# Turning the attention's probabilities on VectorE, in blocks of 32 by 32, in a two-layer decoder trunk

## The chip, the core and the metric

The kernel runs on one core of a Trainium2 chip. The metric is the device time of one execution in microseconds (us), inputs and outputs in the chip's main memory. The kernel before takes 889.86 us, the median of three runs (889.71 to 890.35).

## The reference

One sequence of 512 tokens, width 1024, goes through two layers. The first mixes tokens by causal pooling over windows of 2, 4, 8 and 16 and has a gate. The second is attention with 16 heads of width 64 in three dilation branches (1, 4, 16) that share keys and values projected once; each branch gives an output and a log-denominator, and a softmax over those weighs the three. Each layer ends in a layer norm of `alpha * h + y`.

```python
scores = einsum('bnqrhd,bnkrhd->bnrhqk', qb, kk) * (HEAD_DIM ** -0.5)
scores = where(valid, scores - slope * dilation * rel, NEG_INF)
lse = logsumexp(scores, axis=-1)
p = exp(scores - lse[..., None])
out = einsum('bnrhqk,bnkrhd->bnqrhd', p, vv)          # per branch
...
wts = softmax(stack(lses), axis=0)
merged = sum(wts[..., None] * stack(outs), axis=0)
y = (merged * silu(gate)) @ w_out
```

Scores come out with queries on partitions and keys along the free dimension. The product with the values sums over keys, so the probabilities have to be turned, keys onto partitions, before it. That turning is what the change touches.

## The kernel before

Large products are done in three passes of a rounded type: each operand is split into `hi` and `lo`, and TensorE computes hi x hi, hi x lo and lo x hi (`project`, L526, matmuls at L534). For each weight tile of 128x1024, SyncE loads `raw`, ScalarE casts `hi` (L114) and VectorE subtracts `lo` (L115), with three buffers for each. One such projection of 128 output rows is 24 matmuls of 128x512. This text calls it a **fill**, because in the attention stage fills stand between the pieces of attention.

The attention stage works on 8 pairs of heads (`Attention`, two heads i = 0, 1). Each pair has two **kinds**: kind 0 is the branch of dilation 1, where a block of 128 queries meets the block of keys before it and its own, and kind 1 is the two dilated branches, where tokens are ordered by residue, so that each block of 128 queries meets 128 keys of its own block twice, once for each branch. In the branch of dilation 16 only the four blocks of 32 by 32 on the diagonal are not masked.

- `scores(kind)` (L601 on TensorE): 4 PSUM tiles `sc` of tag "sc" (4 buffers). VectorE's custom operation (L609) adds the mask to `sc`, writes `e` and its row minimum, 8 times; ScalarE takes the exponential in place and the sum (L613), 8 times. In kind 0 two of the eight cover 128 keys, the others 256.
- `transposed(kind, bb)`: turns `e`. In kind 0 TensorE transposes 6 (bb = 0) or 8 (bb = 1) squares of 128x128 into `tp` (L639) and ScalarE copies them to `eT` (L642). In kind 1 TensorE transposes the 4 squares of the branch of dilation 4 (L625), ScalarE copies them into `diag` (L626), and VectorE **turns** the diagonal blocks of the branch of dilation 16 with `transpose`, which turns each block of 32 by 32 (L630, four blocks in one operation).
- `values(kind)` (L655): the products with the values, into the PSUM tile `o`, copied by ScalarE to `o_sb`.
- `weigh` (VectorE; matmul `pm`), `turn` (transpose `ft`, `rows`, `rows_r`) and `spread` (two matmuls `fp`, L707, two multiplications of `o_sb` by `fp`, L709, and their sum `num`): the weights of the branches.

The PSUM tag "tp" has two buffers, and `tp`, `o` and `fp` take turns in them; an allocation waits until the tile two places earlier has been read. The orders of TensorE and SyncE are written out by hand; those of VectorE, ScalarE and GpSimd come from a scheduler that places each instruction by its own estimate of when it can run. Each engine runs its own queue in order. Step n of the loop below does: values of step n-2, scores of step n, then three fills, with the transposes of step n-1 between them and the pair's weights spread in the odd steps. A pair is two steps. The first 48 fills make keys and queries of all pairs and branches (`key_query`, L543; a `k` is copied from PSUM by ScalarE, L549, a `q` by VectorE with its scale, L552); the last 7 are gates, whose PSUM tile three VectorE passes read or follow (L565, L567, L570).

```python
for n in range(2 * NPAIR + 1):
    if n >= 2: heads[n // 2 - 1].values(n % 2)
    if n < 2 * NPAIR: heads[n // 2].scores(n % 2)
    next(fill)(done.turn if done else nothing)
    heads[(n - 1) // 2].transposed((n - 1) % 2, 0)
    next(fill)(nothing)
    heads[(n - 1) // 2].transposed((n - 1) % 2, 1)    # after kind 1: weigh()
    next(fill)(done.spread if done else nothing)
```

Of the kernel before, what the change touches and what calls it, by code (L numbers as in the profile page):

```python
# [8 lines left out]
F32 = mybir.dt.float32  # L9
F32R = mybir.dt.float32r  # L10
BF16 = mybir.dt.bfloat16
AF = mybir.ActivationFunctionType
# [3 lines left out]
P = 128  # L16
S = 512
# [3 lines left out]
NT = S // P  # L21
# [6 lines left out]
HD = 64  # L28
# [41 lines left out]
def trunk(ctx, tc, x, w_in_a, w_grp_a, scale_a, w_out_a, w_kv, w_in_b, w_out_b, ln_g, ln_b, tab, out):  # L70
    nc = tc.nc
    x = x[0]
# [11 lines left out]
    ps = ps_ab.enter_context(tc.tile_pool(name="ps_m", bufs=1, space=PSUM))  # L84
# [8 lines left out]
    ident = const.tile([P, P], F32, name="ident")  # L93
# [76 lines left out]
    with ExitStack() as pa:  # L170
# [135 lines left out]
        for half in range(2):  # L306
            acc = out_proj(ps_y, "y", 4, lambda k, tok: (a_hi[:, k, tok], a_lo[:, k, tok]), w_out_a, half)
            for t in acc:
                tok = slice(t * P, (t + 1) * P)
                h = layer_norm_rows(ap_, acc[t], xr[t], gb[:, 0], gb[:, 1])  # L310
                for kq in range(2):
                    tp = (ps, ps_y)[half].tile([P, 4, P], F32, name="tp", tag=("mm", "y")[half], bufs=4)
# [15 lines left out]
    with ExitStack() as pb:  # L328
# [4 lines left out]
        t_q, to_token, block, residue, qsc, row_block, spread_to = (tabs[:, e - n:e] for e, n in zip(ends, sizes))  # L333
# [4 lines left out]
        v_sb = [(v0s[p], v12s[p][:, 0], v12s[p][:, 1]) for p in range(NPAIR)]  # L338
# [176 lines left out]

        spread_r = qk.tile([P, 2, P], F32R, name="spread_r")
        nc.scalar.copy(spread_r, spread_to.rearrange("p (k m) -> p k m", k=2))
        diag = [qk.tile([P, 2, 2, 256], F32, name="diag", tag="diag", bufs=2) for _ in range(2)]
        for t in diag:
            nc.gpsimd.memset(t, 0.0)  # L520
        wide = []
        for _ in range(2):
# [20 lines left out]
        def key_query(pair, g, j):  # L543
            def emit(mid):
                pt = project((w_kv_v, w_in_v)[j][:, :, g * D + pair * P:g * D + (pair + 1) * P], mid)
                t = qk.tile([P, S], F32, name="kq"[j], tag="kq"[j], bufs=6)
                dst, src = shaped(g, t, pt)
                if j == 0:
                    nc.scalar.copy(dst, src)  # L549
                else:  # L550
                    c = 2 * pair + min(g, 1)
                    nc.vector.tensor_scalar_mul(dst, src, qsc[:, c:c + 1])  # L552
                kq[pair, g, j] = t
            return emit

# [18 lines left out]
        class Attention:  # L574
# [5 lines left out]
            def __init__(self, pair):  # L580
                self.pair = pair

                self.st = sm.tile([P, 2, NT, 4], F32, name="st", tag="st", bufs=2)
                self.own = sm.tile([P, NT, 4], F32, name="own", tag="own", bufs=2)
                self.e, self.eT, self.o = {}, {}, {}

            def scores(self, kind):
                pair = self.pair
                for bb in range(2):
                    sc = [ps_s.tile([P, 2, 256], F32, name="sc", tag="sc", bufs=4) for _ in range(2)]  # L590
                    first = [P * (kind == 0 and bb == 0 and j == 0) for j in range(2)]
                    for j in range(2):
                        b = 2 * bb + j
                        blk = slice(b * P, (b + 1) * P)
                        for g in ((0,), (1, 2))[kind]:
                            for i in range(2):
                                rows = slice(i * HD, (i + 1) * HD)
                                f = first[j]
                                dst, keys = ((sc[i][:, j, f:], slice((b - 1) * P + f, (b + 1) * P)) if g == 0 else
                                             (sc[i][:, j, (g - 1) * P:g * P], blk))  # L600
                                nc.tensor.matmul(dst, kq[pair, g, 1][rows, blk], kq[pair, g, 0][rows, keys],  # L601
                                                 start=True, stop=True)
                    stats = (self.st[:, 0], self.own)[kind]
                    self.e[kind, bb] = es = qk.tile([P, 2, 2, 256], F32, name="e", tag="e", bufs=4)
                    for i in range(2):
                        e = es[:, i]
                        for j in range(2):
                            b, f = 2 * bb + j, first[j]
                            nc.vector.tensor_tensor_reduce(  # L609
                                e[:, j, f:], sc[i][:, j, f:], t_q[:, kind * 256 + f:(kind + 1) * 256],  # L610
                                -SLOPES[2 * kind][2 * pair + i], 3e38, op0=ALU.add, op1=ALU.min,
                                accum_out=stats[:, b, i:i + 1])
                            nc.scalar.activation(e[:, j, f:], e[:, j, f:], AF.Exp, bias=stats[:, b, i:i + 1],  # L613
                                                 scale=-1.0, accum_out=stats[:, b, 2 + i:3 + i])

            def transposed(self, kind, bb):
                es = self.e.pop((kind, bb))
                if kind == 1:

                    t = diag[bb]  # L620
                    tp = ps.tile([P, 2, 2, P], F32, name="tp", tag="tp", bufs=2)
                    for i in range(2):
                        self.eT[kind, bb, i] = t[:, i].rearrange("p j c -> p (j c)")
                        for j in range(2):
                            nc.tensor.transpose(tp[:, i, j], es[:, i, j, 0:P], ident)  # L625
                    nc.scalar.copy(t.rearrange("p i j c -> p (i j) c")[:, :, 0:P], tp.rearrange("p i j c -> p (i j) c"))  # L626
                    for s in range(4):
                        q = slice(32 * s, 32 * (s + 1))
                        cols = slice(P + 32 * s, P + 32 * (s + 1))
                        nc.vector.transpose(t[q].rearrange("p i j c -> p (i j) c")[:, :, cols],  # L630
                                            es[q].rearrange("p i j c -> p (i j) c")[:, :, cols])
                    return
                for i in range(2):
                    e = es[:, i]
                    tp = ps.tile([P, S], F32, name="tp", tag="tp", bufs=2)

                    parts = [e[:, 0, P:], e[:, 1, 0:P], e[:, 1, P:]] + [e[:, 0, 0:P]] * bb
                    for c, part in enumerate(parts):
                        nc.tensor.transpose(tp[:, c * P:(c + 1) * P], part, ident)  # L639
                    n = len(parts) * P  # L640
                    self.eT[kind, bb, i] = t = qk.tile([P, S], F32, name="eT", tag="eT", bufs=4)
                    nc.scalar.copy(t[:, 0:n], tp[:, 0:n])  # L642

            def values(self, kind):
                o = ps.tile([P, S], F32, name=f"o{kind}", tag="tp", bufs=2)
                for bb in range(2):
                    b = 2 * bb

                    if kind == 0:
                        parts = [(0, b, 0, b, 2), (0, b + 1, 2, b + 1, 1)] + [(0, b - 1, 3, b, 1)] * bb  # L650
                    else:
                        parts = [(1 + g, b + j, 2 * j + g, b + j, 1) for j in range(2) for g in range(2)]
                    for n, (g, kb, c, qb, w) in enumerate(parts):
                        for i in range(2):
                            nc.tensor.matmul(o[i * HD:(i + 1) * HD, qb * P:(qb + w) * P], v_sb[self.pair][g][:, kb, i],  # L655
                                             self.eT[kind, bb, i][:, c * P:(c + w) * P],
                                             start=(bb == 0 and n == 0), stop=(bb == 1 and n == len(parts) - 1))
                self.o[kind] = o_sb = qk.tile([P, S], F32, name="o_sb", tag=f"o{kind}", bufs=1)
                if kind == 0:
                    nc.scalar.copy(o_sb, o)  # L660
                else:
                    nc.scalar.copy(o_sb.rearrange("p (a s r) -> p a s r", s=4, r=4),
                                   o.rearrange("p (r s a) -> p a s r", r=4, s=4))
# [27 lines left out]
            def turn(self):  # L691

                ft = ps_s.tile([P, S], F32, name="ft", tag="sc", bufs=4)
                nc.tensor.transpose(ft[:, 0:P], wide[self.pair % 2], ident)
                rows = qk.tile([P, NT, P], F32, name="rows", tag="rows", bufs=1)
                nc.vector.tensor_mul(rows, ft[:, 0:P].unsqueeze(1).broadcast_to([P, NT, P]),
                                     row_block.unsqueeze(2).broadcast_to([P, NT, P]))
                self.rows = qk.tile([P, NT, P], F32R, name="rows_r", tag="rows_r", bufs=1)
                nc.scalar.copy(self.rows, rows)
                nc.vector.tensor_sub(self.rows[32:48], rows[32:48], self.rows[32:48])  # L700
# [129 lines left out]
```

## Time and profile before

| | |
|---|---|
| median of the runs shown | 889.86 us |
| the profiled execution | 889.12 us, of which the trace's span is 887.3 |
| TensorE matmul busy | 876.3 us (99%), granted clock 0.999 |
| VectorE busy | 527.8 us (59%) |
| ScalarE busy | 369.4 us (42%) |
| GpSimd busy | 13.1 us (1%) |
| attention stage | from 441.7 us, one pair of heads every 43.80 us |

The rows further down come from six views. The page gives shares over the whole span; the windows give the busy time of each engine in one stretch; the chain in order of time says what the end waited for, piece by piece; the groups by form give the mean duration of one kind of instruction on one shape; and the timelines show instructions of one engine with their starts. TensorE's matmuls overlap, so the time that one costs is read from starts or from the chain's pieces, not from its duration. In the chain a piece counts records, and a product of two plain 32-bit operands leaves two records per instruction where `o` and `sc` are concerned.

### The profile page before, as it was taken

The page shows a single profiled execution, that of the slowest core. Times are in us where ns is not written, and L with a number is a line of the kernel's source. Part 1 is how long each engine was busy: PE and PEld are TensorE (multiplying, and loading weights), DVE is VectorE, ACT ScalarE, POOL GpSimd, SP SyncE. Part 2 cuts the span into 40 slices and gives each one's busy share as a digit, 9 for nine tenths or more (in the row PEclk, how much of TensorE's full clock was granted, in tenths as well). Part 3 has the DMA queues.
Part 4 walks back from the last instruction along what each step waited for, and adds up shares of the span by engine and source line. Part 5 has one row for each costly group of instructions (what it writes and reads, how often), then busy time and mean ns, then how long its engine had stood idle before and what let it go on. Part 6 is the DMA issues. An engine that isn't in the chain of part 4 may idle for free.

```text
span 887.3 us, 11570 instructions
## 1 busy us (share of the span) xinstructions
PE 876.3 (99%) x4499; PEld 717.2 (81%) x4499; DVE 527.8 (59%) x968; ACT 369.4 (42%) x699; POOL 13.1 (1%) x65
## 2 busy tenths in 40 slices
PE   9999999999999999999999999999999999999996
PEld 6888888888887877788888888888888888888885
DVE  3756466584549489879534454545454545465665
ACT  3633333333433425554543444444444444454410
POOL 0000000000000000000000000000000000000000
PEclk9999999999999999999999999999999999999999
DMA  7533434333455644352233222222222222223261
GB/s 226 177 96 96 144 94 148 103 104 98 142 193 188 217 164 138 119 168 66 64 107 95 72 72 72 72 72 72 72 73 72 72 72 72 72 72 95 72 214 71
DMA packets 112855, 97.70 MB, mean 110 GB/s; under 512 B 5152, under 2 KB 97312, under 8 KB 112800
## 3 DMA queue, kind: packets, MB, share of 16 engines
q1 hardware_dynamic: 112080, 94.39, 34.3%
q10 hardware_dynamic: 720, 2.57, 0.8%
q8 instruction: 35, 0.57, 0.3%
q14 instruction: 20, 0.16, 0.1%
HBM read 92.76 MB, written 4.19 MB: 109 GB/s over the span
## 4 chain that ended last, share of the span: by engine, by line
PE 94%; DVE 3%; issue 1%; ACT 0%; DMA 0%; DVEq 0%
PE mm L534 35%; PE y L145 9%; PE mm L127 6%; PE mm L126 6%; PE mm L128 6%; PE yb L729 5%; PE vy L468 4%; PE sc L601 3%; PE v L390 3%; PE o L655 3%; PE mm L224 3%; PE vz L468 2%; PE mx L126 2%; PE mx L127 2%; PE mx L128 2%; PE tp L639 1%
## 5 line engine op out<-in xcount | busy, mean ns | idle before, releaser
L115 DVE TENSOR_TENSOR lo<-raw,hi 128x1024 fp32r<-128x1024 f32 (+1 forms) x148 | 176.2, 1194 | 210.2 <-ACT hi L114 203.7
L114 ACT CAST hi<-raw 128x1024 fp32r<-128x1024 f32 (+1 forms) x148 | 151.7, 1029 | 307.8 <-issue 140.0
L534 PE MATMUL mm<-hi_T,hi 128*128 128x512 f32 x448 | 180.6, 403 | 0.0
L534 PE MATMUL mm<-hi_T,lo 128*128 128x512 f32 x448 | 175.3, 391 | 0.0
L534 PE MATMUL mm<-lo_T,hi 128*128 128x512 f32 x448 | 174.6, 390 | 0.0
L534 PEld LDWEIGHTS mm<-hi_T,hi 128*128 128x128 f32 x448 | 84.2, 188 | 20.3 <-issue 3.0
L534 PEld LDWEIGHTS mm<-hi_T,lo 128*128 128x128 f32 x448 | 84.1, 188 | 18.5
L534 PEld LDWEIGHTS mm<-lo_T,hi 128*128 128x128 f32 x448 | 84.4, 188 | 16.0
L127 PE MATMUL mm<-lo_T,hi 128*128 128x512 f32 x224 | 87.2, 389 | 0.0
L128 PE MATMUL mm<-hi_T,lo 128*128 128x512 f32 x224 | 87.2, 389 | 0.0
L126 PE MATMUL mm<-hi_T,hi 128*128 128x512 f32 x224 | 87.2, 389 | 0.0
L128 PEld LDWEIGHTS mm<-hi_T,lo 128*128 128x128 f32 x224 | 42.0, 188 | 8.8
L126 PEld LDWEIGHTS mm<-hi_T,hi 128*128 128x128 f32 x224 | 42.0, 188 | 8.8
L127 PEld LDWEIGHTS mm<-lo_T,hi 128*128 128x128 f32 x224 | 42.0, 188 | 8.6
L609 DVE CUSTOM_DVE_ANT_0 e<-sc,tabs 128x256 f32<-128x256 f32 (+1 forms) x128 | 43.3, 403 | 7.9 <-PE sc L601 7.9
L552 DVE TENSOR_SCALAR q<-mm,tabs 128x512 f32<-128x512 f32 x24 | 18.0, 751 | 46.2 <-PE mm L534 46.0
L145 PE MATMUL y<-lo,a_hi 128*128 128x512 f32 x128 | 39.9, 390 | 0.5 <-DVE lo L115 0.5
L145 PE MATMUL y<-hi,a_hi 128*128 128x512 f32 x128 | 39.9, 392 | 0.4 <-DVE x_tok L154 0.4
L145 PE MATMUL y<-hi,a_lo 128*128 128x512 f32 x128 | 39.7, 389 | 0.0
L729 PE MATMUL yb<-hi,a_b 128*128 128x512 f32 x128 | 39.7, 389 | 0.0
L359 DVE TENSOR_TENSOR lo<-b,hi 128x1024 fp32r<-128x1024 f32 x24 | 29.4, 1223 | 13.6 <-ACT hi L358 13.4
L358 ACT CAST hi<-b 128x1024 fp32r<-128x1024 f32 x24 | 25.3, 1055 | 26.1 <-PE vy L468 15.6
(175 smaller groups left out, 1329.1 us busy)
## 6 DMA issues: line engine op xcount, KB each, us to landing
raw<-in_w_out_a_dram SPq DMA_DIRECT2D x32, 512.0 KB, 3.3
raw<-in_w_kv_dram SPq DMA_DIRECT2D x32, 512.0 KB, 3.8
raw<-in_w_in_b_dram SPq DMA_DIRECT2D x32, 512.0 KB, 3.8
raw<-in_w_in_a_dram SPq DMA_DIRECT2D x28, 512.0 KB, 3.9
b<-in_w_kv_dram SPq DMA_DIRECT2D x16, 512.0 KB, 4.6
raw<-in_w_grp_a_dram SPq DMA_DIRECT2D x8, 512.0 KB, 3.6
raw<-in_w_out_b_dram SPq DMA_DIRECT2D x8, 512.0 KB, 3.3
x_col<-in_x_dram SPq DMA_DIRECT2D x4, 512.0 KB, 7.2
```

Of the source, the lines that this page charges most:

```text
L114: nc.scalar.copy(hi[:, parts[i]], raw[:, parts[i]])
L115: nc.vector.tensor_sub(lo[:, parts[i]], raw[:, parts[i]], hi[:, parts[i]])
L126: nc.tensor.matmul(ps, lh, rh, start=(i == 0), stop=False)
L127: nc.tensor.matmul(ps, lh, rl, start=False, stop=False)
L128: nc.tensor.matmul(ps, ll, rh, start=False, stop=(i == n - 1))
L145: nc.tensor.matmul(acc[t][c], l, r[:, 0, c * 512:(c + 1) * 512], start=(k == 0 and s == 0), stop=(k == nk - 1 and s == 2))
L224: nc.tensor.matmul(pts[i], l[:, kk, f], xT[r][:, k], start=(k == 0 and n == 0), stop=(k == NK - 1 and n == 2))
L359: nc.vector.tensor_sub(dst[1], src, dst[0])
L468: nc.tensor.matmul(acc[:, i], lhs[l][:, 2 * (n % 2) + kk, i], w[r][:, kk], start=(begins and kk == 0 and s == 0), stop=(n % 2 == 1 and kk ...
L534: nc.tensor.matmul(pt, l[:, k], hT[r][:, k], start=(k == 0 and n == 0), stop=(k == NK - 1 and n == 2))
L609: nc.vector.tensor_tensor_reduce(e[:, j, f:], sc[i][:, j, f:], t_q[:, kind * 256 + f:(kind + 1) * 256], -SLOPES[2 * kind][2 * pair + i], 3 ...
L729: nc.tensor.matmul(acc[t, c], a_b[k][:, l, tok], ws[k][r][:, 0, cs], start=(k == 0 and n == 0), stop=(k == NK - 1 and n == 2))
```

## The change

`e` and `eT` become four tiles that live through the whole stage, one of each per kind, with both heads and all four query blocks in them (128x2048). All squares are now turned by VectorE's `transpose` and written straight to `eT`. A helper `turn(q, k, ...)` takes the 32 partitions of block row q and the 32 columns of block column k, for all squares at once, turns each block and writes it to the 32 partitions k at the columns q. In kind 0 the first half turns the own-block squares with k <= q (10 operations over 8 squares), the second half the squares of the block before with k >= q (10 over 7). Blocks that the mask leaves empty are not turned; `eT` is cleared once by GpSimd. In kind 1 the 12 operations off the diagonal cover 8 squares of the branch of dilation 4, and the 4 on the diagonal cover both branches, 16. The tiles `tp` and `diag` go, with their transposes on TensorE and copies on ScalarE. The copy of a `q` from PSUM goes to ScalarE as an activation with a scale.

```diff
         spread_r = qk.tile([P, 2, P], F32R, name="spread_r")
         nc.scalar.copy(spread_r, spread_to.rearrange("p (k m) -> p k m", k=2))
-        diag = [qk.tile([P, 2, 2, 256], F32, name="diag", tag="diag", bufs=2) for _ in range(2)]
-        for t in diag:
+        e_t = [qk.tile([P, 2, NT, 256], F32, name="e", tag="e", bufs=2) for _ in range(2)]
+        eT_t = [qk.tile([P, 2, NT, 256], F32, name="eT", tag="eT", bufs=2) for _ in range(2)]
+        nc.gpsimd.memset(e_t[0][:, :, 0, 0:P], 0.0)
+        for t in eT_t:
...
                     nc.scalar.copy(dst, src)
                 else:
                     c = 2 * pair + min(g, 1)
-                    nc.vector.tensor_scalar_mul(dst, src, qsc[:, c:c + 1])
+                    nc.scalar.activation(dst, src, AF.Copy, scale=qsc[:, c:c + 1])
                 kq[pair, g, j] = t
...
                 self.own = sm.tile([P, NT, 4], F32, name="own", tag="own", bufs=2)
-                self.e, self.eT, self.o = {}, {}, {}
+                self.o = {}
             def scores(self, kind):
...
                     for i in range(2):
-                        e = es[:, i]
                         for j in range(2):
                             b, f = 2 * bb + j, first[j]
+                            e = e_t[kind][:, i, b, f:]
                             nc.vector.tensor_tensor_reduce(
-                                e[:, j, f:], sc[i][:, j, f:], t_q[:, kind * 256 + f:(kind + 1) * 256],
+                                e, sc[i][:, j, f:], t_q[:, kind * 256 + f:(kind + 1) * 256],
                                 -SLOPES[2 * kind][2 * pair + i], 3e38, op0=ALU.add, op1=ALU.min,
                                 accum_out=stats[:, b, i:i + 1])
-                            nc.scalar.activation(e[:, j, f:], e[:, j, f:], AF.Exp, bias=stats[:, b, i:i + 1],
+                            nc.scalar.activation(e, e, AF.Exp, bias=stats[:, b, i:i + 1],
                                                  scale=-1.0, accum_out=stats[:, b, 2 + i:3 + i])
-            def transposed(self, kind, bb):
-                es = self.e.pop((kind, bb))
+            def transposed(self, kind, half):
+                e, t = (x[kind].rearrange("p i b c -> p (i b) c") for x in (e_t, eT_t))
+                def turn(q, k, cols, rows, src, dst):
+                    q, k = (slice(32 * x, 32 * (x + 1)) for x in (q, k))
+                    nc.vector.transpose(dst[k][:, :, rows + q.start:rows + q.stop],
+                                        src[q][:, :, cols + k.start:cols + k.stop])
                 if kind == 1:
-                    t = diag[bb]
-                    tp = ps.tile([P, 2, 2, P], F32, name="tp", tag="tp", bufs=2)
-                    for i in range(2):
-                        self.eT[kind, bb, i] = t[:, i].rearrange("p j c -> p (j c)")
-                        for j in range(2):
-                            nc.tensor.transpose(tp[:, i, j], es[:, i, j, 0:P], ident)
-                    nc.scalar.copy(t.rearrange("p i j c -> p (i j) c")[:, :, 0:P], tp.rearrange("p i j c -> p (i j) c"))
-                    for s in range(4):
-                        q = slice(32 * s, 32 * (s + 1))
-                        cols = slice(P + 32 * s, P + 32 * (s + 1))
-                        nc.vector.transpose(t[q].rearrange("p i j c -> p (i j) c")[:, :, cols],
-                                            es[q].rearrange("p i j c -> p (i j) c")[:, :, cols])
+                    both = [x[1].rearrange("p i b (g c) -> p (i b g) c", g=2) for x in (e_t, eT_t)]
+                    for q in (2 * half, 2 * half + 1):
+                        for k in range(4):
+                            turn(q, k, 0, 0, *(both if q == k else (e, t)))
                     return
-                for i in range(2):
-                    e = es[:, i]
-                    tp = ps.tile([P, S], F32, name="tp", tag="tp", bufs=2)
-                    parts = [e[:, 0, P:], e[:, 1, 0:P], e[:, 1, P:]] + [e[:, 0, 0:P]] * bb
-                    for c, part in enumerate(parts):
-                        nc.tensor.transpose(tp[:, c * P:(c + 1) * P], part, ident)
-                    n = len(parts) * P
-                    self.eT[kind, bb, i] = t = qk.tile([P, S], F32, name="eT", tag="eT", bufs=4)
-                    nc.scalar.copy(t[:, 0:n], tp[:, 0:n])
+                for q in range(4):
+                    for k in range(4):
+                        if half == 0 and k <= q:
+                            turn(q, k, P, 0, e, t)
+                        elif half == 1 and k >= q:
+                            turn(q, k, 0, P, e[:, 1:], t[:, 0:-1])
             def values(self, kind):
                 o = ps.tile([P, S], F32, name=f"o{kind}", tag="tp", bufs=2)
-                for bb in range(2):
-                    b = 2 * bb
-                    if kind == 0:
-                        parts = [(0, b, 0, b, 2), (0, b + 1, 2, b + 1, 1)] + [(0, b - 1, 3, b, 1)] * bb
-                    else:
-                        parts = [(1 + g, b + j, 2 * j + g, b + j, 1) for j in range(2) for g in range(2)]
-                    for n, (g, kb, c, qb, w) in enumerate(parts):
-                        for i in range(2):
-                            nc.tensor.matmul(o[i * HD:(i + 1) * HD, qb * P:(qb + w) * P], v_sb[self.pair][g][:, kb, i],
-                                             self.eT[kind, bb, i][:, c * P:(c + w) * P],
-                                             start=(bb == 0 and n == 0), stop=(bb == 1 and n == len(parts) - 1))
+                if kind == 0:
+                    parts = [(0, 0, 0, 0, 2), (0, 1, 0, 1, 1), (0, 2, 0, 2, 2), (0, 3, 0, 3, 1), (0, 1, P, 2, 1)]
+                else:
+                    parts = [(1 + g, b, g * P, b, 1) for b in range(NT) for g in range(2)]
+                for n, (g, b, c, qb, w) in enumerate(parts):
+                    for i in range(2):
+                        nc.tensor.matmul(o[i * HD:(i + 1) * HD, qb * P:(qb + w) * P], v_sb[self.pair][g][:, b, i],
+                                         eT_t[kind][:, i, b, c:c + w * P],
+                                         start=(n == 0), stop=(n == len(parts) - 1))
                 self.o[kind] = o_sb = qk.tile([P, S], F32, name="o_sb", tag=f"o{kind}", bufs=1)
                 if kind == 0:
```

VectorE, a middle pair, from the last score operation of kind 1 to the multiplication by `fp` (rows of 128x1 are its sums). Before:

```order
453 L630 STREAM_TRANSPOSE diag<-e 32x4x32 x6
454 L696 TENSOR_TENSOR rows<-ft,tabs 128x512
455 L630 STREAM_TRANSPOSE diag<-e 32x4x32 x2
456 L669 TENSOR_TENSOR x<-own,tabs 128x64
457 L700 TENSOR_TENSOR rows_r<-rows,rows_r 16x512
458 L552 TENSOR_SCALAR q<-mm,tabs 128x512
459 L115 TENSOR_TENSOR lo<-raw,hi 128x1024 x2
460 L709 TENSOR_TENSOR o_sb<-o_sb,fp 128x512 x2
461 L711 TENSOR_TENSOR num<-o_sb 128x512
462 L552 TENSOR_SCALAR q<-mm,tabs 128x512
463 L115 TENSOR_TENSOR lo<-raw,hi 128x1024
```

VectorE, the same place in the new order, from `rows_r` on (ahead of these rows, behind the last score operation, stand one turn of 32x16x32, `rows` and three turns of 32x8x32):

```order
470 L696 TENSOR_TENSOR rows_r<-rows,rows_r 16x512
471 L625 STREAM_TRANSPOSE eT<-e 32x8x32
472 L625 STREAM_TRANSPOSE eT<-e 32x16x32
473 L625 STREAM_TRANSPOSE eT<-e 32x8x32
474 L115 TENSOR_TENSOR lo<-raw,hi 128x1024
475 L625 STREAM_TRANSPOSE eT<-e 32x8x32 x3
476 L625 STREAM_TRANSPOSE eT<-e 32x16x32
477 L625 STREAM_TRANSPOSE eT<-e 32x8x32 x4
478 L625 STREAM_TRANSPOSE eT<-e 32x16x32
479 L665 TENSOR_TENSOR x<-own,tabs 128x64
480 L115 TENSOR_TENSOR lo<-raw,hi 128x1024
481 L705 TENSOR_TENSOR o_sb<-o_sb,fp 128x512 x2
```

Eight turns of 32x4x32 stood ahead of `x`; now sixteen larger ones stand ahead of it, with one `lo` among them, and the copy of `q` that stood ahead of `lo` is gone. Both orders come to the multiplication of `o_sb` by `fp` after them.

TensorE, a middle pair, between the second and the third fill behind kind 1's scores, with tile numbers (`mm_4590` and `mm_4637` are the two fills). Before:

```order
L534 MATMUL mm_4590<-hi_T_1833,hi_4585 128x512
L534 MATMUL mm_4590<-lo_T_1834,hi_4585 128x512
L534 MATMUL mm_4590<-hi_T_1833,lo_4586 128x512
L639 MATMUL tp_4617<-ident_83,e_4329 128x128 x4
L639 MATMUL tp_4624<-ident_83,e_4329 128x128 x4
L534 MATMUL mm_4637<-hi_T_1833,hi_4632 128x512
L534 MATMUL mm_4637<-lo_T_1834,hi_4632 128x512
```

TensorE, the same place in the new order (fills `mm_4559` and `mm_4602`):

```order
L538 MATMUL mm_4559<-hi_T_1833,hi_4554 128x512
L538 MATMUL mm_4559<-lo_T_1834,hi_4554 128x512
L538 MATMUL mm_4559<-hi_T_1833,lo_4555 128x512
L538 MATMUL mm_4602<-hi_T_1833,hi_4597 128x512
L538 MATMUL mm_4602<-lo_T_1834,hi_4597 128x512
```

The transposes into `tp` that stood between the fills are gone, and nothing stands in their place.

VectorE, the last pair, where fills are gates (`sgb` and `a_b` are their tiles), up to the multiplication by `fp`. Before:

```order
733 L630 STREAM_TRANSPOSE diag<-e 32x4x32 x4
734 L700 TENSOR_TENSOR rows_r<-rows,rows_r 16x512
735 L669 TENSOR_TENSOR x<-own,tabs 128x64
736 L115 TENSOR_TENSOR lo<-raw,hi 128x1024
737 L565 SCALAR_TENSOR_TENSOR sgb<-sgb,mm 128x512
738 L567 SCALAR_TENSOR_TENSOR sgb<-num,sgb 128x512
739 L570 TENSOR_TENSOR a_b<-sgb,a_b 128x512
740 L115 TENSOR_TENSOR lo<-raw,hi 128x1024
741 L565 SCALAR_TENSOR_TENSOR sgb<-sgb,mm 128x512
742 L567 SCALAR_TENSOR_TENSOR sgb<-num,sgb 128x512
743 L709 TENSOR_TENSOR o_sb<-o_sb,fp 128x512
```

VectorE, the same place in the new order (ahead of it stand `rows`, two turns, `rows_r`, four turns and a `lo`):

```order
792 L569 SCALAR_TENSOR_TENSOR sgb<-sgb,mm 128x512
793 L625 STREAM_TRANSPOSE eT<-e 32x8x32
794 L571 SCALAR_TENSOR_TENSOR sgb<-num,sgb 128x512
795 L625 STREAM_TRANSPOSE eT<-e 32x8x32 x3
796 L574 TENSOR_TENSOR a_b<-sgb,a_b 128x512
797 L625 STREAM_TRANSPOSE eT<-e 32x16x32
798 L625 STREAM_TRANSPOSE eT<-e 32x8x32
799 L115 TENSOR_TENSOR lo<-raw,hi 128x1024
800 L569 SCALAR_TENSOR_TENSOR sgb<-sgb,mm 128x512
801 L625 STREAM_TRANSPOSE eT<-e 32x8x32
802 L571 SCALAR_TENSOR_TENSOR sgb<-num,sgb 128x512
803 L705 TENSOR_TENSOR o_sb<-o_sb,fp 128x512 x2
```

The passes of two gates stood ahead of the multiplication; now turns stand between them, and three more come after it.

## Rows read from the trace of the kernel before

**Rows 1.** The page: parts 1, 2 (clock by slice), 4 (chain).

```profile
PE 876.3 (99%) x4499; PEld 717.2 (81%) x4499; DVE 527.8 (59%) x968; ACT 369.4 (42%) x699; POOL 13.1 (1%) x65
...
PEclk9999999999999999999999999999999999999999
...
PE 94%; DVE 3%; issue 1%; ACT 0%; DMA 0%; DVEq 0%
```

**Rows 2.** Windows, two pairs of heads: us, then busy time by engine, clock.

```profile
678.80:722.60 43.80, 43.80 (x273) 35.86 (x274) 22.26 (x65) 20.34 (x51) 0.00 (x0) 1.00 0.25 73
...
766.40:810.20 43.80, 43.80 (x272) 35.86 (x273) 26.47 (x72) 23.21 (x56) 0.00 (x0) 1.00 0.25 73
```

**Rows 3.** Chain in order of time, attention stage: start us, us, engine, tile, line.

```profile
441.72 16.32 PE mm L534 x72
...
686.15 0.44 PE tp L625 x4
686.59 5.50 PE mm L534 x24
692.08 0.44 PE tp L625 x4
692.52 0.17 PE pm L672 x2
692.69 5.54 PE mm L534 x24
...
700.13 1.99 PE sc L601 x32
...
707.96 0.66 PE tp L639 x6
708.61 5.50 PE mm L534 x24
714.11 0.87 PE tp L639 x8
714.98 2.74 PE mm L534 x12
717.72 0.45 PE fp L707 x2
...
720.89 1.67 PE o L655 x20
...
787.73 1.99 PE sc L601 x32
```

**Rows 4.** Groups by form: line engine op out<-in xcount | busy, mean ns | idle.

```profile
L630 DVE STREAM_TRANSPOSE diag<-e 32x128 f32<-32x128 f32 x64 | 19.3, 302 | 4.6 <-ACT e L613 3.9
L609 DVE CUSTOM_DVE_ANT_0 e<-sc,tabs 128x256 f32<-128x256 f32 x112 | 40.5, 420 | 5.2 <-PE sc L601 5.2
L609 DVE CUSTOM_DVE_ANT_0 e<-sc,tabs 128x128 f32<-128x128 f32 x16 | 4.6, 288 | 2.8 <-PE sc L601 2.8
L687 DVE TENSOR_TENSOR wide<-f,m 128x16 f32<-128x16 f32 x16 | 2.1, 172 | 0.4
L552 DVE TENSOR_SCALAR q<-mm,tabs 128x512 f32<-128x512 f32 x24 | 18.0, 751 | 46.2 <-PE mm L534 46.0
L549 ACT COPY k<-mm 128x512 f32<-128x512 f32 x24 | 13.9, 579 | 0.0
```

**Rows 5.** Timeline of VectorE, one pair: start us, us, operation.

```profile
704.01 1.25 DVE L630 STREAM_TRANSPOSE diag<-e 32x128 f32<-32x128 f32 x4
...
706.45 0.69 DVE L696 TENSOR_TENSOR rows<-ft,tabs 128x512 f32<-128x512 f32 x1
...
709.47 1.22 DVE L115 TENSOR_TENSOR lo<-raw,hi 128x1024 fp32r<-128x1024 f32 x1
```

**Rows 6.** Timeline of ScalarE, a middle pair and the last: start us, us.

```profile
705.59 0.19 ACT L613 ACTIVATION_READ_ACCUMULATOR e<-e,own 128x1 f32 x1
...
793.95 0.19 ACT L613 ACTIVATION_READ_ACCUMULATOR e<-e,own 128x1 f32 x1
```

More of the change, by code (lines that the diff above doesn't have):

```diff
@@ L603, in scores @@
                     stats = (self.st[:, 0], self.own)[kind]
-                    self.e[kind, bb] = es = qk.tile([P, 2, 2, 256], F32, name="e", tag="e", bufs=4)
                     for i in range(2):
-                        e = es[:, i]
                         for j in range(2):
                             b, f = 2 * bb + j, first[j]
+                            e = e_t[kind][:, i, b, f:]
                             nc.vector.tensor_tensor_reduce(
-                                e[:, j, f:], sc[i][:, j, f:], t_q[:, kind * 256 + f:(kind + 1) * 256],
+                                e, sc[i][:, j, f:], t_q[:, kind * 256 + f:(kind + 1) * 256],
```

## The prediction

> **What bounds the kernel now.** I read the page's first parts, the windows, the chain in order of time, the groups by form, and then the timelines of VectorE and ScalarE. TensorE is busy for 876.3 of 887.3 us, at a granted clock of nine tenths or more in all 40 slices, and it holds 94% of the chain that ended last [rows 1]. [...]
>
> **What TensorE loses.** A fill (24 projection matmuls) takes 16.32 / 3 = 5.44 us when nothing stands before it [rows 3]. Per pair four groups of transposes stand between fills: 0.44, 0.44, 0.66 and 0.87 us, together 2.41, and the fill behind each runs longer than its 5.44 (or 2.72 for half of one): 5.50, 5.54, 5.50 and 2.74 [rows 3]. Of these tails, 0.06 + 0.10 + 0.06 + 0.02, the second also has pm in front of it, which stays; I leave half of that one to pm. That makes 2.41 + 0.19 = 2.60 us per pair, and 8 pairs give 20.8 us; without the tails it is 8 x 2.41 = 19.3, the lower bound. Everything else on TensorE keeps its count: values has 10 matmuls in kind 0 and 16 in kind 1 before and after, with the same widths. Scores, pm, ft, fp are untouched.
>
> **What VectorE gains and loses.** It loses 8 old turns of 302 ns and 3 copies of q of 751 ns per pair [rows 4], 4.7 us. It gets 20 turns in kind 0 (10 of 32x8x32, 10 of 32x7x32) and 16 in kind 1 (12 of 32x8x32, 4 of 32x16x32). The trace has only turns of 128 elements per lane. From them I price the others with the slope of the scores' operation, 420 - 288 = 132 ns for 128 more elements [rows 4]: 302 + 132 = 434 ns for 256 elements, 401 for 224, 698 for 512. The bounds: with no slope at all every turn would take 302; with a start-up no dearer than that of a tiny operation (172 ns for 16 elements, so about 156 for none [rows 4]) the slope is 146 per 128, giving 448 and 740; and with no start-up, everything proportional, 256 elements cost 604, 224 cost 529 and 512 cost 1208. I take 434, nearest to a measured slope, and keep the proportional price for a rival. [...]
>
> Four old turns in a row take 1.25 us [rows 5], so each starts only after the one before it ended, with some 14 ns between; the scores' operation overlaps its neighbours and the turns do not. So I add 14 ns to each: kind 0 costs 10 x 0.448 + 10 x 0.415 = 8.6 us, kind 1 costs 12 x 0.448 + 4 x 0.712 = 8.2 us. VectorE then has 22.26 - 4.7 + 16.8 = 34.4 us of work in a pair of 43.80 - 2.60 = 41.2 us: 83%. Full on average it is not; but it is one queue in order, so I follow it through the pair.
>
> **The tight place: kind 1.** The changed order puts all sixteen turns of kind 1 directly behind that kind's score operations, waiting for the last exponential, and in front of the multiplication of o_sb by the first fp. That multiplication frees the buffer of tag "tp" that the next pair's kind 0 output needs (two buffers serve o, o, fp, fp in turn), so TensorE's o waits for it. Before, only 8 short turns stood there. Count from the start of kind 1's scores on TensorE, at 700.13 [rows 3]. The last exponential's sum is read at 705.59 + 0.19 [rows 6], 5.65 after it. Then VectorE has the turns, 8.2; rows and rows_r, 0.72 each with the gap [rows 5]; x, about 0.25 (172 ns and the slope for 48 more elements); two lo, 1.23 each [rows 5]; and the multiplication, 0.69 as rows takes: 13.1 us. It ends 18.75 after the scores' start, with 0.1 for the semaphore 18.85. TensorE reaches o at 720.89 - 700.13 = 20.76 before, and now 1.61 sooner (0.66 + 0.06 + 0.87 + 0.02), at 19.15. So o finds its buffer free with 0.3 us to spare. At the upper start-up bound (448 and 740) the turns take 0.34 longer and nothing is left. I price the stall of the six ordinary pairs (the first has no fp) at zero.
>
> **The last pair** has gates as fills, with three VectorE passes each, and there the cover is gone. By the new order 10 turns of 256 and 3 of 512 stand between the exponentials and that multiplication (6.6 us), with rows_r, two lo, and four passes over sgb and one over a_b at about 0.70 each, and the multiplication: 6.6 + 0.72 + 2.46 + 3.5 + 0.69 = 14.0. The exponentials end at 793.95 + 0.19 [rows 6], 6.41 after the scores' start at 787.73 [rows 3]; 6.4 + 14.0 + 0.1 = 20.5 against 19.15: o waits 1.3 us. I charge this.
>
> **The other half, kind 0**, has more room. Counted from its scores' start, the exponentials end no later than kind 1's do (5.65, two of the eight being half as wide), then come 8.6 us of turns, two lo (2.5) and some ten small operations of 0.2: 18.7 until VectorE reaches the third lo. That one has to wait for the end of the third fill (the scores and 16.32, over 18 us) and then for ScalarE's hi, about 1 us, in any case; kind 1's scores start on time. The lo are made long before they are read: the one at 709.47 [rows 5] belongs to the fill behind the next pair's first scores, after 720.89 + 1.67 [rows 3], 13 us later. The new order makes it some 3 us later, and the DMA that refills its raw as well; 10 us stay as cover.
>
> **q's copies on ScalarE** take 579 ns as k's do [rows 4], 3 x 0.58 = 1.7 us per pair; and six copies of tp (four of 128x512, two of 128x384) go, so ScalarE, at 20.34 of 43.80 [rows 2], gets lighter. No copy of q is read sooner than a fill after it. GpSimd clears two tiles of 128x2048 in place of two of 128x1024, and a small one, several fills ahead of the first turn. Both cost nothing.
>
> **Sum**, against the profiled execution's own 889.12 (span 887.3): 889.12 - 20.8 + 1.3 = 869.6. The median of the runs shown is 889.86, 0.74 above it, so I forecast 870.3.
>
> **Rivals.**
> A (0.62) is the forecast; its own range is 869 to 873 (the tails' bound adds 1.5, a stall of 0.2 per pair 1.2).
>
> B (0.22): TensorE's wait at o comes in every pair. For it speaks the 0.3 us to spare, out of 19; against it that the price rests on slopes that VectorE shows. With turns of 256 at 484 (50 more, the 512 three times that) kind 1 grows by 24 x 0.05 = 1.2 us; 1.2 - 0.3 = 0.9 per pair, six times, and 0.95 more in the last: 870.3 + 5.4 + 0.95 = 876.7. It spans 873 to 889.
>
> C (0.08): VectorE becomes the bound and the kernel is slower. The place is the same o, the price the proportional one: kind 1 grows by 12 x 0.170 + 4 x 0.510 = 4.1, of which 3.8 is a stall; kind 0 by 10 x 0.170 + 10 x 0.128 = 3.0, of which 0.5 gets past its room; 4.3 a pair, six times, and 3.2 + 0.5 in the last: 870.3 + 25.8 + 3.7 = 899.8. It decides from a turn of about 565 ns: 131 more, for which six pairs at 24 x 0.131 - 0.3 and the last at 19 x 0.131 eat the 19.5 that the forecast gains. Against it speaks that a start-up of nothing is unlike any row of VectorE: 16 elements cost 172 ns. A transpose of 128x128 costs TensorE 0.87 / 8 = 0.11 us [rows 3] and by the sum above VectorE 16.8 / 22 = 0.76, but TensorE is the one without idle time. [...]
>
> D (0.08): nothing of the gain is lost, not even in the last pair, because the scheduler's order leaves more slack than I counted, or the turns are cheaper than 434: 868.3 + 0.74 = 869.0. No more is to be had from TensorE than the 2.60 per pair.
>
> **How the numbers follow.** Within 0.2%, 1.8 us, is about what a measurement of this kernel cannot tell from no change. Faster takes A, D and nearly all of B: 0.90; B's upper end near 889 gives same 0.03; C gives slower 0.07. The range starts below D at 868.3 and reaches through most of B, to 880; it leaves out B's tail and C.
>
> **What would show it.** Right: a pair's window of 41.2 us with TensorE busy throughout, VectorE near 34 us, turns of 434, 401 and 698 ns, and one wait of about 1.3 us on the multiplication by fp, in the last pair. Wrong: turns above 460 ns, or o waiting on that multiplication in each pair (B); a pair longer than 43.8 us with VectorE busy in all of it (C); or TensorE waiting for lo or hi, which I priced at nothing.

## The result, and the profile after

The changed kernel takes 870.58 us, the median of four runs from 870.10 to 870.84, beside 889.88 for the kernel before: a ratio of 0.9782, 95% interval 0.9765 to 0.9799. The forecast was 870.3. The profiled execution took 870.47 us with a span of 868.7, against 889.12 and 887.3. Of all runs below one is left out of its kernel's numbers: one of e6 took 1072.84 us at a mean granted clock of 0.752, where the others show 0.997 to 0.999.

The page first, its parts 1, 2 (clock by slice) and 4 (chain), to be held against [rows 1]:

```profile
PE 857.0 (99%) x4323; PEld 700.4 (81%) x4323; DVE 621.1 (72%) x1168; ACT 361.7 (42%) x675; POOL 15.0 (2%) x66
...
PEclk9999999999999999999999999999999999999998
...
PE 94%; DVE 4%; issue 1%; ACT 0%; DVEq 0%
```

TensorE is as full as before, with 176 matmul records fewer, which is the number of 128x128 transposes that went (22 a pair), and 19.3 us less busy time. VectorE has 93 us more work, and the chain gives it 4% of a shorter span in place of 3%. The windows of two ordinary pairs and of the 41.26 us behind them, in which the last pair's scores fall (us, then busy time of TensorE, its weight loads, VectorE, ScalarE and GpSimd, the granted clock, DMA share, GB/s) answer to [rows 2]:

```profile
665.77:707.03 41.26, 41.26 (x252) 33.63 (x253) 33.90 (x90) 19.39 (x49) 0.00 (x0) 1.00 0.27 77
707.03:748.29 41.26, 41.26 (x252) 33.63 (x253) 33.91 (x90) 19.39 (x49) 0.00 (x0) 1.00 0.27 77
748.29:789.55 41.26, 41.26 (x250) 33.56 (x249) 35.70 (x91) 20.23 (x50) 0.00 (x0) 1.00 0.28 78
```

A pair takes 41.26 us in place of 43.80, all of it TensorE's at a granted clock of 1.00, as before. So TensorE waits for nothing in these stretches, although VectorE's share went from 22.26 / 43.80 = 51% to 33.90 / 41.26 = 82%. The chain in order of time shows what went and what came (start us, us, what); it answers to [rows 3]:

```profile
710.42 11.11 PE mm L538 x48
721.53 0.17 PE pm L668 x2
721.69 5.54 PE mm L538 x24
727.24 1.90 PE o L651 x32
729.14 1.99 PE sc L605 x32
...
734.19 10.93 PE mm L538 x48
745.12 0.45 PE fp L703 x2
745.57 2.72 PE mm L538 x12
748.29 1.67 PE o L651 x20
...
770.40 1.99 PE sc L605 x32
...
790.07 0.61 DVE o_sb L705
790.68 0.04 issue
790.72 1.74 PE o L651 x20
```

Where `tp` stood four times a pair, two fills now follow each other as one piece: 11.11 us for 48 matmuls in place of 5.67, 0.44, 5.50 and 0.44; the first of these is the fill behind kind 0's scores before:

```profile
680.48 5.67 PE mm L534 x24
```

In the last pair alone the chain leaves TensorE before `o`. The stage as a whole is counted from the start of its first fill to the start of the long piece `yb` in the chain, here first before and then after:

```profile
838.82 40.92 PE yb L729 x180
```

```profile
442.16 16.32 PE mm L538 x72
...
820.18 40.91 PE yb L725 x180
```

The first fill of before starts at 441.72 [rows 3], so the stage takes 397.10 us before and 378.02 after, 19.08 less. The list of TensorE's waits (who waits for whom: us in total, times, longest) has the wait at `o` once in the whole execution, and TensorE's timeline gives its size:

```profile
PE o L651 <- DVE o_sb L705: 1.2, 1, 1.2
```

```profile
790.72 1.74 PE L651 MATMUL o<-eT,v 128*64 128x256 f32 x20 [1.17 <-DVE o_sb L705]
```

The list has no row of L538, so no fill waits for `lo` or `hi`.

The groups by form price what came, against [rows 4]:

```profile
L625 DVE STREAM_TRANSPOSE eT<-e 32x256 f32<-32x256 f32 x176 | 76.8, 436 | 16.1 <-ACT e L616 13.4
...
L625 DVE STREAM_TRANSPOSE eT<-e 32x224 f32<-32x224 f32 x80 | 32.2, 403 | 1.2
L625 DVE STREAM_TRANSPOSE eT<-e 32x512 f32<-32x512 f32 x32 | 22.5, 703 | 13.0 <-ACT e L616 12.7
...
L556 ACT ACTIVATE q<-mm,tabs 128x512 f32<-128x512 f32 x24 | 16.3, 680 | 0.0
L553 ACT COPY k<-mm 128x512 f32<-128x512 f32 x24 | 13.8, 576 | 0.0
```

The turns cost 436, 403 and 703 ns, where 434, 401 and 698 were forecast. The copy of a `q` costs 680 ns, where 579 was forecast, the price of a `k`.

Last the tight place, VectorE in an ordinary pair after kind 1's scores, which start at 729.14 (start us, us, operation, [idle before]; a row that holds several turns mixes their sizes under the first one's); it answers to [rows 5]:

```profile
734.81 0.70 DVE L625 STREAM_TRANSPOSE eT<-e 32x512 f32<-32x512 f32 x1 [1.71 <-ACT e L616]
735.44 0.64 DVE L692 TENSOR_TENSOR rows<-ft,tabs 128x512 f32<-128x512 f32 x1
736.11 1.34 DVE L625 STREAM_TRANSPOSE eT<-e 32x256 f32<-32x256 f32 x3
737.48 0.68 DVE L696 TENSOR_TENSOR rows_r<-rows,rows_r 16x512 fp32r<-16x512 f32 x1
738.19 1.60 DVE L625 STREAM_TRANSPOSE eT<-e 32x256 f32<-32x256 f32 x3
739.82 1.22 DVE L115 TENSOR_TENSOR lo<-raw,hi 128x1024 fp32r<-128x1024 f32 x1
741.08 4.58 DVE L625 STREAM_TRANSPOSE eT<-e 32x256 f32<-32x256 f32 x9
745.67 0.23 DVE L665 TENSOR_TENSOR x<-own,tabs 128x64 f32<-128x64 f32 x1
745.81 1.22 DVE L115 TENSOR_TENSOR lo<-raw,hi 128x1024 fp32r<-128x1024 f32 x1
746.95 1.27 DVE L705 TENSOR_TENSOR o_sb<-o_sb,fp 128x512 f32<-128x512 f32 x2
```

All sixteen turns, `rows`, `rows_r`, `x` and two `lo` stand ahead of the first multiplication by `fp`, as the prediction listed them. One such multiplication takes 0.68 us in the mean, so it ends at 746.95 + 0.68 = 747.63, which is 18.49 after the scores' start, and TensorE reaches `o` at 19.15: 0.66 us to spare.

### The profile page after: what moved, and what is told of

It is laid out like the page before. It is cut to its first block, busy times and chain, and to the rows that moved or that the text cites. A ratio compares the mean times of both kernels' runs of the same rounds, so it can differ in the third digit from the quotient of the medians.

```text
span 868.7 us, 11406 instructions
## 1 busy us (share of the span) xinstructions
PE 857.0 (99%) x4323; PEld 700.4 (81%) x4323; DVE 621.1 (72%) x1168; ACT 361.7 (42%) x675; POOL 15.0 (2%) x66
## 4 chain that ended last, share of the span: by engine, by line
PE 94%; DVE 4%; issue 1%; ACT 0%; DVEq 0%
PE mm L538 34%; PE y L145 9%; PE mm L128 6%; PE mm L127 6%; PE mm L126 6%; PE yb L725 5%; PE v L390 5%; PE vy L468 4%; PE sc L605 3%; PE o L651 3%; PE mm L224 3%; PE vz L468 3%; PE mx L128 2%; PE mx L127 2%; PE mx L126 2%
## 5 line engine op out<-in xcount | busy, mean ns | idle before, releaser
L538 PE MATMUL mm<-hi_T,hi 128*128 128x512 f32 x448 | 178.1, 398 | 0.0
L538 PE MATMUL mm<-hi_T,lo 128*128 128x512 f32 x448 | 174.8, 390 | 0.0
L538 PE MATMUL mm<-lo_T,hi 128*128 128x512 f32 x448 | 174.4, 389 | 0.0
L625 DVE STREAM_TRANSPOSE eT<-e 32x256 f32<-32x256 f32 (+2 forms) x288 | 131.5, 457 | 30.3 <-ACT e L616 26.0
L538 PEld LDWEIGHTS mm<-hi_T,hi 128*128 128x128 f32 x448 | 84.1, 188 | 21.1 <-issue 2.8
L538 PEld LDWEIGHTS mm<-hi_T,lo 128*128 128x128 f32 x448 | 84.1, 188 | 18.1
L538 PEld LDWEIGHTS mm<-lo_T,hi 128*128 128x128 f32 x448 | 84.2, 188 | 16.6
```

What stands on the lines that cost most here:

```text
L538: nc.tensor.matmul(pt, l[:, k], hT[r][:, k], start=(k == 0 and n == 0), stop=(k == NK - 1 and n == 2))
L625: nc.vector.transpose(dst[k][:, :, rows + q.start:rows + q.stop], src[q][:, :, cols + k.start:cols + k.stop])
```

## The experiments

Two questions were left. Is it this place that limits what the change may cost VectorE, or is it VectorE's load as a whole? And what is each part of the change worth?

**A dose at the tight place (e6).** Four of kind 1's turns are made a second time, with the same result; VectorE gets some 1.8 us more per pair, ahead of the multiplication.

```diff
+                            if k == (q + 1) % 4:
+                                turn(q, k, 0, 0, e, t)
```

> The changed kernel, with four of kind 1's turns of 32x8x32 done twice in each pair (1.8 us more on VectorE per pair). Theory (in order, o waits for the multiplication behind the turns; 0.56 us to spare, from 747.63 and 748.29 less the semaphore): a stall of 1.8 - 0.56 = 1.24 us in each of six pairs, 7.4 us; in the last pair the scheduler puts the multiplication one pass over sgb earlier, 0.7 less; together 877.3 us. Rival (VectorE has 41.26 - 33.9 = 7.4 us idle in a pair, so 1.8 more are hidden): 870.6.

Measured: 878.91 us (878.52 to 879.13, three runs), ratio 0.9879 (0.9859 to 0.9899), 1.6 us over the expectation. The list of TensorE's waits, and then in its timeline the `o` behind the pair that was shown above:

```profile
PE o L653 <- DVE o_sb L707: 8.9, 7, 1.4
```

```profile
757.08 1.74 PE L653 MATMUL o<-eT,v 128*64 128x256 f32 x20 [1.42 <-DVE o_sb L707]
```

The wait now comes seven times, in every pair that has an `fp` before it (the last time 0.3 us, where the order puts the multiplication one pass over `sgb` earlier). The chain of this kernel tells why (at 736.51 kind 1's scores start, and in the middle of them the chain leaves TensorE):

```profile
714.32 1.74 PE o L653 x20
...
736.51 1.14 PE sc L605 x16
...
756.43 0.61 DVE o_sb L707
757.08 1.74 PE o L653 x20
```

A pair takes 757.08 - 714.32 = 42.76 us, 1.50 more than in the changed kernel, where 1.24 was expected; six times the difference is the 1.6 us. The wait is 1.42 of it, and `o` itself takes 1.74 us in place of 1.67. The multiplication ends at 757.04, 20.53 after the scores, where it was 18.49 in the changed kernel: 2.04 later, not 1.79. Of the other 0.25 some 0.15 is in how the scheduler placed the neighbours: the second `lo` now stands ahead of the last long turn, and what overlapped before (`lo` with `x` by 0.09 us and with the multiplication by 0.08) no longer does. The rest is in small gaps between turns: three take 1.37 us in place of 1.34, and the twelve between the two `lo`, one of them long, 5.71, where 11 x 0.436 + 0.703 and eleven gaps of 0.014 make 5.65. Of the 2.04 the 0.66 to spare are hidden, and 1.38 is left; with the 0.04 between the multiplication's end and `o` that is the 1.42 of the row.

**The same dose elsewhere (e5).** The four extra turns go into kind 0, whose half was said to have room.

```diff
+                            if k == q:
+                                turn(q, k, P, 0, e, t)
```

> The changed kernel, with four of kind 0's turns of 32x8x32 done twice in each pair (the same 1.8 us more on VectorE per pair). Theory (behind kind 0's turns VectorE idles 1.6 us before the third lo and 0.9 before kind 1's scores anyway, and no tile of TensorE is held by them): no change, 870.6 us. Rival (VectorE's work as such sets the pace): as much as the dose in kind 1, about 877; and if all of it showed, 885.

Measured: 870.88 us (870.80 to 870.94), ratio 0.9787 (0.9773 to 0.9802), and in the list of TensorE's waits the one wait at `o`:

```profile
PE o L653 <- DVE o_sb L707: 1.3, 1, 1.3
```

An ordinary pair takes 41.26 us in its chain (`o` at 707.29 and at 748.55), as in the changed kernel, with VectorE busy for 35.56 of them. The stage takes 820.62 - 442.41 = 378.21 us, 0.19 more, and the last pair's wait has grown by as much (1.35 for 1.17 in the timeline). So thirty-two turns of 436 ns, 14 us of VectorE's time, cost 0.2 us there; at the tight place they cost 8. VectorE's load as a whole limits nothing here; its queue at one place does.

**The buffer taken away (e7).** The matmuls `fp` write to the scores' buffers instead of those of "tp", so the next `o` need not wait until `fp` is read. The last pair's own keeps its place, as no `o` follows it.

```diff
-            def spread(self):
+            def spread(self, pool=ps_s, tag="sc", bufs=4):
...
-                    fp = ps.tile([P, S], F32, name="fp", tag="tp", bufs=2)
+                    fp = pool.tile([P, S], F32, name="fp", tag=tag, bufs=bufs)
...
-                last.spread()
+                last.spread(ps, "tp", 2)
```

> The changed kernel, with fp in a buffer of tag sc in place of tp (not in the last gate's spread), so that the next o does not wait for the multiplication by fp. VectorE's order stays as it is. Theory (TensorE is the bound and waits for VectorE only at that o, only in the last pair, 1.17 us): 870.6 - 1.2 = 869.4 us, and no wait of TensorE on o_sb in the trace. Rival (what holds the last pair is VectorE's amount of work, not that buffer): the wait moves to another tile of the last pair and the time stays at 870.6.

Measured: 869.34 us (868.65 to 869.74), ratio 0.9769 (0.9755 to 0.9784). In TensorE's timeline the last pair's `o` stands without a wait, and VectorE's order in the stage is that of the changed kernel:

```profile
789.48 1.74 PE L651 MATMUL o<-eT,v 128*64 128x256 f32 x20
```

**Buffer and dose together (e8),** the edits of e6 and e7 in one kernel.

> The dose of four more turns in kind 1, with fp in a buffer of tag sc. VectorE's order is that of the dose alone. Theory (the stall of the dose comes from the tp buffer that o needs): the 1.8 us are hidden, 869.4 us. Rival (the stall comes from VectorE's being late for something else, scores or lo): near 877.

Measured: 869.25 us (869.10 to 869.39), ratio 0.9769 (0.9754 to 0.9784), no wait at `o`. The dose that cost 8 us costs nothing once `fp` is elsewhere: the price was the shared buffer, not the turns.

**The copies of q alone (e1),** in the kernel before.

```diff
-                    nc.vector.tensor_scalar_mul(dst, src, qsc[:, c:c + 1])
+                    nc.scalar.activation(dst, src, AF.Copy, scale=qsc[:, c:c + 1])
```

> The kernel before, with only q's copies moved to ScalarE. Theory (TensorE is the bound and no copy of q is read sooner than a fill after it): no change, 889.9 us. Rival (part of the gain comes from taking the copies off VectorE): below 889.

Measured: 889.57 us beside 889.62, ratio 0.9998 (0.9988 to 1.0007): nothing, within some 0.1%. The stage takes 839.37 - 442.26 = 397.11 us in its chain, where it was 397.10.

**The turns alone (e2),** the changed kernel with `q` copied by VectorE (the same two lines, the other way).

> The changed kernel, with q's copies on VectorE again (0.75 us each, three per pair). By the new order one of them stands among kind 1's turns, ahead of the multiplication by fp: 0.67 us more there against 0.56 to spare. Theory: a stall of 0.1 to 0.2 us in six pairs, 871.3 to 871.8 us. Rival (the copies matter for themselves, all three of a pair): up to 8 x 2 us more, 887.

Measured: 871.12 us (870.85 to 871.28), ratio 0.9792 (0.9776 to 0.9808), a little under the 871.3 to 871.8 that was expected; from the changed kernel itself it can't be told by these intervals. The trace is clearer: the first multiplication (in VectorE's timeline) ends at 748.08 + 0.68 = 748.76, and `o` (in the chain) starts 0.06 us later.

```profile
748.08 1.28 DVE L705 TENSOR_TENSOR o_sb<-o_sb,fp 128x512 f32<-128x512 f32 x2
```

```profile
748.82 1.74 PE o L651 x20
```

One copy of `q` there eats all that was to spare, and the pair takes 41.37 us (the `o` before it starts at 707.45) in place of 41.26. The stage takes 820.78 - 442.10 = 378.68 us, 0.66 more than in the changed kernel, which is six times 0.11. So the second part of the change has no value by itself and a small one beside the first: it keeps the slack.

**One kind alone (e3: kind 0, e4: kind 1).** In each, one kind (`VK`, 0 in e3 and 1 in e4) is turned by VectorE as in the changed kernel and the other keeps TensorE's transposes and ScalarE's copies. The lines shown are e3's.

```diff
+        VK = 0
...
+                if kind != VK:
+                    bb = half
+                    es = self.e.pop((kind, bb))
...
+                            nc.tensor.transpose(tp[:, i, j], es[:, i, j, 0:P], ident)
```

> Only kind 0 is turned by VectorE; kind 1 goes as in the kernel before (transposes on TensorE, diagonal blocks on VectorE). q's copies on ScalarE. Theory (what TensorE no longer does comes off the end): kind 0's transposes with their tails are 1.61 us a pair, 8 x 1.61 = 12.9, so 877.0 us, and no wait at o, since only eight short turns stand ahead of it. Rival (the gain is lost where VectorE has 17 us less room): above 880.

> Only kind 1 is turned by VectorE; kind 0 goes as in the kernel before. q's copies on ScalarE. Theory: kind 1's transposes are 0.88 us a pair with 0.06 to 0.11 of tails, 8 x 0.95 = 7.6, so 882.3 us. TensorE comes to o 1.6 us later than in the changed kernel, so the last pair does not wait. The two halves' gains, 12.9 and 7.6, should add up to the change's 19.3 plus the 1.17 us of stall. Rival (kind 1's sixteen turns make o wait): above 884.

Measured: e3 876.74 us (876.66 to 876.92), ratio 0.9856 (0.9841 to 0.9871); e4 883.68 us (883.61 to 883.96), ratio 0.9934 (0.9919 to 0.9949). The period of a pair, between two starts of kind 0's `o` in the chain of e3 and then of e4:

```profile
711.92 1.67 PE o L686 x20
...
754.11 1.67 PE o L686 x20
```

```profile
716.75 1.67 PE o L673 x20
...
759.62 1.67 PE o L673 x20
```

These are 42.19 and 42.87 us: kind 0 saves 1.61 per pair, kind 1 saves 0.93, and 1.61 + 0.93 is the 2.54 of both. e3 came as expected. e4 is 1.4 us over its expectation, and I was wrong there: I had said that its last pair would not wait. It does, for 1.19 of those 1.4 us, as VectorE's timeline and then TensorE's show:

```profile
799.73 1.22 DVE L115 TENSOR_TENSOR lo<-raw,hi 128x1024 fp32r<-128x1024 f32 x1
800.88 0.68 DVE L568 SCALAR_TENSOR_TENSOR sgb<-sgb,mm 128x512 f32<-128x512 f32 x1
801.59 0.71 DVE L638 STREAM_TRANSPOSE eT<-e 32x512 f32<-32x512 f32 x1
802.33 0.69 DVE L570 SCALAR_TENSOR_TENSOR sgb<-num,sgb 128x512 f32<-128x512 f32 x1
802.93 1.28 DVE L733 TENSOR_TENSOR o_sb<-o_sb,fp 128x512 f32<-128x512 f32 x2
```

```profile
803.67 1.74 PE L673 MATMUL o<-eTs,v 128*64 128x256 f32 x20 [1.19 <-DVE o_sb L733]
```

I had counted 13 turns ahead of that multiplication, the order of the changed kernel. In e4 the scheduler put all 16 there, three more, and the multiplication ends at 802.93 + 0.68 = 803.61, 21.9 us after the scores (at 781.72 in the chain), where it was 20.3 in the changed kernel. TensorE's transposes of kind 0 give `o` 1.6 us more time there, and the order takes them back.

**The changed kernel and e7 side by side,** once more and on one chip, since 1.2 us is near what two measurements apart can tell (e9 is the changed kernel without an edit, e10 is e7).

> The changed kernel once more, beside the version whose gates' sums (fp) go through the scores' buffers, so that the two are timed on the same chip. Theory (fp holds a buffer that the next pair's o needs, and only the last pair pays for it): 870.6 us, one wait of TensorE at o of about 1.2 us, in the last pair. Rival (the 1.2 us between the two kernels was the difference of two calls): the two come out within 0.3 us of each other.

> The gates' sums in the scores' buffers, otherwise the changed kernel. Theory: 869.4 us, 1.2 us under the changed kernel of the same call, no wait of TensorE at o. Rival: within 0.3 us of the changed kernel.

Measured: 870.47 us (870.21 to 870.69, five runs) and 869.32 (869.27 to 869.35, four runs), ratios 0.9785 (0.9771 to 0.9798) and 0.9772 (0.9758 to 0.9785) to the kernel before. The two ranges lie apart, 1.15 us between the medians, and the trace has one wait of 1.2 us in the first and none in the second. e7 beats both kernels, by 0.13% the changed one.

## Why the prediction was right

- **What TensorE loses:** TensorE has all 43.80 us of a pair before [rows 2] and all 41.26 after, so what it no longer does comes off the pair. 2.60 us per pair were forecast, 43.80 - 41.26 = 2.54 measured, between the lower bound (2.41, no tails) and the value taken. The tails were real, and 0.06 of them too many were counted: the fill behind `pm` takes 5.54 after as before, so that tail, of which half was counted, stays whole. Eight pairs give 20.3, where 20.8 was charged.
- **The price of a turn:** within 5 ns for all three sizes. The slope that was borrowed from another VectorE operation (132 ns for 128 elements) holds for the turn: 436 - 302 = 134, and (703 - 436) / 2 = 133.5. That settles rival C, whose proportional price would have been 604 and 1208.
- **VectorE's load:** 34.4 us of a pair forecast, 33.9 measured.
- **The tight place:** the exponentials end 5.65 after the scores as forecast from [rows 6] (the turn that waits for them starts at 734.81, 5.67 after). From there 12.8 us in place of 13.1, since `rows`, `lo` and the multiplication overlap their neighbours by 0.07 to 0.09 us each, which the sum did not take off. The 0.1 us that the sum takes for the semaphore, as do the last pair's sum and the 0.56 to spare of e6 and e2, is an estimate of mine that no run shows; the chain has 0.04 (790.68 to 790.72). So 0.66 us to spare in place of 0.3, or 0.62 with the semaphore, and the ordinary pairs stall for nothing, as charged. That the place is the right one is shown, not argued: the same dose costs 8 us there (e6), 0.2 in kind 0 (e5) and nothing without the shared buffer (e8). Rival B was one small cost away: e2 sits on the edge, e6 beyond it.
- **The last pair:** 1.3 us charged, 1.17 measured; removing it gives 1.15 (e9, e10). Rival D (869.0, no stall) is what e7 reaches by another buffer.
- **q on ScalarE:** priced "as k's", 579 ns, and it is 680. This was the one price that missed, and it cost nothing, as ScalarE works 19.4 of 41.26 us (e1 shows no effect at all). The 680 ns are 680 - 576 = 104 more than the plain copy of a `k`, and 92 and 89 more than the activations of that size from PSUM whose scale is not one value per partition (L262 588, L568 591).
- **The sum:** 20.3 - 1.17 = 19.1 from the stage's rows, and 19.08 measured for the stage as a whole, where the forecast took off 20.8 - 1.3 = 19.5. The medians differ by 19.3. The two profiled executions differ by 18.65, since the stages ahead ended 0.44 later in the one of after. That is no effect of the change: of the other executions that of the changed kernel in e9 starts its first fill at 441.92, and that of e1, with the attention of before, at 442.26.

By work VectorE is the dearer place (76.8 + 32.2 + 22.5 = 131.5 us for 176 squares, 0.75 each with the diagonal blocks of dilation 16 in it, against 0.87 / 8 = 0.11 on TensorE [rows 3]), by time it was the free one, as it had half of each pair idle (22.26 of 43.80 us busy [rows 2]) and TensorE nothing.

## What to carry to other kernels

When one engine bounds and another is half idle, even work that the second does seven times slower (here 0.75 us a square against 0.11) can belong there; price it by the order of that engine's queue, not by its load. Look for the instruction in that queue on which the bounding engine waits, count what is placed ahead of it and compare with when it is needed: here 0.66 us of slack decided between nothing and a wait in every pair. And before trimming the queue, ask why it is waited for at all: another PSUM buffer for `fp` took the wait of 1.17 us away (e7) and hid the whole dose (e8).

## What was not expected of the hardware

- Each turn starts only after the turn before it has ended, as the prediction read from four old ones, and the rows of the tight place show it for the larger ones too: three fill a row of 1.34 us (3 x 0.436 and two gaps of 0.014) or, one of them long, of 1.60, while `rows`, `lo` and the multiplications start up to 0.09 us before their neighbour's end. The cost of a turn over the three sizes and the old one (302, 403, 436 and 703 ns for 128, 224, 256 and 512 elements of a lane) fits 168 ns and 1.045 ns per element.
- The copy of a `q`, an activation with a scale per partition, takes 680 ns on ScalarE where the plain copy of a `k`, of the same 128x512 from PSUM, takes 576.
